# Matmuls that read their moving operand alternately from the two halves of its tile

## The chip, the core and the metric

The kernel runs on one core of a Trainium2 chip. The metric is the device time of one execution in microseconds (us); the kernel before was run three times. A core has five engines that work side by side and wait for each other through semaphores: TensorE (PE; its weight loads, PEld, overlap its matmuls), VectorE (DVE), ScalarE (ACT), GpSimd (POOL) and SyncE (SP), which here issues all transfers. Matmul results go to PSUM, eight banks of 512 float32 values in each of 128 partitions; all other tiles lie in SBUF.

## What is computed

A two-layer network on 1024 tokens with 1024 channels, in float32. Layer 0 mixes with sliding-window attention, layer 1 with a gated linear recurrence (HGRN2); a squared-ReLU feed-forward part follows each.

```python
def sqrelu_mlp(h, w_up, w_down):
    return jnp.square(jax.nn.relu(h @ w_up)) @ w_down

def reference(x, positions, ...):
    ...
    for layer in range(DEPTH):
        h = rmsnorm(x, mix_norm[layer])
        if layer % N_MIXERS == 0:
            y = sliding_window_attention(h, positions, ...)   # h @ w_qkv + b, rotary, band of 128, @ w_o
        else:
            y = hgrn2_recurrence(h, lbs[layer], ...)          # h @ w_in, scan over chunks, @ w_o
        x = x + y
        h = rmsnorm(x, mlp_norm[layer])
        x = x + sqrelu_mlp(h, mlp_w_up[layer], mlp_w_down[layer])
    return rmsnorm(x, final_norm)
```

The feed-forward weights are 1024 x 4096 and 4096 x 1024, the recurrence's input weights 1024 x 4096.

## The kernel before

**Layout.** Activations are held transposed: a tile has 128 channels on the partitions and 512 tokens (half of the 1024, index `hf`) in the free dimension. Weights come in blocks of 128 x 512 (`wr`).

**Products in three parts.** A large product is done in float32r, a form of float32 that TensorE takes with fewer bits. `weight_split` and `split` cut each operand into a high part (a cast) and a low part (the difference), and `mm3` adds three matmuls in one PSUM bank: high x high, high x low and low x high. In most products the weights are the stationary operand (128 x 128, names `wh` and `wl`) and the activations the moving one (128 x 512, names `a` or `t`); in the qkv projection it is the other way round, and there the bank has tokens on its partitions and the 512 output channels as its columns.

**Fewer products.** Up projection, down projection and the recurrence's input projections are 2 x 2 block products in the form with seven products (`strassen_weights`, `finish`, `operands`); `product` runs one with 4 x 3 matmuls. Partial sums stay in a bank and are read in between: by ScalarE (`copy`) into a tile, or by VectorE, which adds a bank to a tile (`tt`). Such reads stand in `pair` (up), `down`, `two` and `two_first` (gates of the recurrence), `o_proj`, `hgrn_out`, `projected` and `keys_values` (qkv). PSUM banks have two tags, `q` and `p`, four banks each.

**The last part.** `down` of the last layer ends with products of 256 tokens at a time, and `final` normalises and stores each quarter as it comes; for such a quarter two tiles of 256 columns go out with one transfer.

**What sets the order.** No engine's order is written by hand. `Schedule.add` records each operation with a cost, and `Schedule.order` plays them through as a list scheduler: of what is ready, the operation of the lowest rank on the engine that is free first. Casts that split operands may go to ScalarE or VectorE, whichever the planner takes to end first. The cost of a matmul is set in `mm` (for 512 columns of float32r: 512 / 2.25 + 4 = 231.6). All operations are issued from one place, so every row of the profile has the same line, and the tiles' names tell them apart: `wr` raw weights, `m` sums of weights, `wh` and `wl` split weights, `a` and `t` activations, `d` a store in DRAM, `q` and `p` PSUM banks, `c` constants.

Of the kernel before, what the change touches and what calls it, by code (L numbers as in the profile page):

```python
# [275 lines left out]


class Net:
    def __init__(self, ctx, tc, io):
# [152 lines left out]
    def sum_squares(self, tiles, n=TH):  # L432
        acc = None
        for x in tiles:
            sq = self.t()[:, :n]
            self.act(sq, x, AF.Square, n)
# [49 lines left out]
    def square_relu(self, m, hf, c, psum):  # L486

        r = self.t()
        if psum:
            self.act(r, c, AF.Relu)  # L490
            self.stt(r, c, 0.0, r, ALU.max, ALU.mult)
        else:
            self.stt(r, c, 0.0, c, ALU.max, ALU.mult)
        self.hid[m, hf] = self.keep(r)
# [86 lines left out]
    def pair(self, m, x):  # L581

        w = self.strassen_weights(*(self.io["up"][self.layer, i] for i in (m, m + MT // 2)))

        def read(ps):
            z = self.t()
            self.copy(z, ps)
            return z

        main, side, own = self.psum("q"), self.psum("q"), self.psum()  # L590
        self.product(main, w[1], x[1], True)
        u1 = read(main)
# [11 lines left out]
        self.tt("DVE", u2, side, u2, ALU.add)  # L604
# [56 lines left out]
    def down(self, cut):  # L661
# [8 lines left out]

        def products(names, ps, ws, start, stop, tokens=slice(0, TH), ms=range(HK)):
            for p in ps:
                for name in names:
                    (wh, wl), (xh, xl) = ws[name, p]
                    for m in ms:
                        out = (main if name in (1, 6, 7, 4) else side)[m][:, tokens]
# [3 lines left out]
                        self.mm3(out, (wh[:, c], wl[:, c]), (xh[:, tokens], xl[:, tokens]), first, p == stop,  # L680
                                 tokens.stop - tokens.start, **more)

# [10 lines left out]

        def scaled_sum(hf, out, z, tokens=slice(0, TH)):

            k = tokens.stop - tokens.start
            u = self.t(tag="m")[:, :k]
            self.tt("DVE", u, z, self.r[hf][:, tokens], ALU.mult, k)
            part = out[:, tokens].only(tokens.start)
            self.tt("any", part, u, part, ALU.add, k)  # L700
# [7 lines left out]
        for m in range(HK):  # L708
            y[0, 0, m], y[1, 1, m] = self.a(), self.a()
            self.copy(y[0, 0, m], main[m])  # L710
        for m in range(HK):
            self.copy(y[1, 1, m], side[m])
        run_pass((6,))
        for m in range(HK):
            u = y[0, 1, m] = self.a()
            self.copy(u, main[m])
        for m in range(HK):
# [3 lines left out]
        for m in range(HK):  # L721
            self.copy(parts[m], main[m])
        for m in range(HK):
# [13 lines left out]
        for m in range(HK):  # L737
            self.copy(parts[m], side[m])
        for m in range(HK):
# [16 lines left out]
        for c in (0, TH // 2):  # L756
            tokens = slice(c, c + TH // 2)
            for m in range(HK):
                products((3,), range(n - held, n), ws, False, n - 1, tokens, [m])
                scaled_sum(1, self.x[m][1], side[m][:, tokens], tokens)  # L760
            yield 1, tokens

# [90 lines left out]
    def projected(self, cg, n, ps, r):  # L853
        if cg == 0:
            self.keys_values(n, ps, r)
        else:
            q = self.a()
            self.stt(q, ps, r, self.bias[cg], ALU.mult, ALU.add)
            self.rope(q, 8, n)
            self.q[n][cg - 1] = q  # L860

    def keys_values(self, n, ps, r):
        W = NG * HD
        k = self.t(F32, (P, W))
        self.stt(k, ps[:, :W], r, self.bias[0][:, :W], ALU.mult, ALU.add, W)
        if n % 2 == 0:
            self.v.append(self.a(F32, (P, 2, W)))
        v = self.v[n // 2][:, n % 2].only(n)
        self.stt(v, ps[:, W:], r, self.bias[0][:, W:], ALU.mult, ALU.add, W)
        if n % 2 == 0:  # L870
# [101 lines left out]
    def o_proj(self, hf, out):  # L972

        a = [self.split(out[g, j]) for g in range(NG) for j in range(2)]
        for m in range(KT):
# [6 lines left out]
            self.x[m][hf] = self.a()  # L982
            self.tt("DVE", self.x[m][hf], ps, x, ALU.add)
            yield
# [61 lines left out]
    def two_first(self, which, e, x):  # L1046

        self.s.lead = LEAD
        w = [self.weight_split(self.raw(self.io["win"][which[0], e][:, c : c + TH])) for c in (0, TH)]
        self.s.lead = 0  # L1050
        main, own, y0 = self.psum(), self.psum(), self.t()
        self.product(main, w[0], x[1], True)
        self.copy(y0, main)
        self.product(own, w[1], x[2], True)
        self.tt("DVE", y0, own, y0, ALU.add)
        return main, y0

    def two(self, which, e, x, out, begun=None):
# [6 lines left out]
        if not begun:  # L1065
            self.product(main, w[1], x[1], True)
            self.copy(y0, main)
        yield
        self.product(side, w[5], x[5], True)
        self.copy(z1, side)  # L1070
        yield
        self.product(main, w[6], x[6], False)
        self.copy(y1, main)
        yield
        if not begun:
            self.product(own, w[2], x[2], True)
            self.tt("DVE", y0, own, y0, ALU.add)
        yield
        self.product(main, w[7], x[7], False)
        self.tt("DVE", z1, main, z1, ALU.add)  # L1080
        yield
        self.product(side, w[3], x[3], False)
        self.tt("DVE", y1, side, y1, ALU.add)
        yield
        self.product(main, w[4], x[4], False)
        self.copy(z0, main)
        yield
# [132 lines left out]
    def hgrn_out(self, hf, y, total):  # L1220
        r = self.t()
        self.copy(r, self.rstd(total, 0.25, 0.25))
        for m in range(KT):
# [6 lines left out]
            z = self.t()  # L1230
            self.tt("DVE", z, ps, r, ALU.mult)
            self.x[m][hf] = self.a()
# [31 lines left out]

    def final(self, hf, tokens=slice(0, TH)):
        n = tokens.stop - tokens.start
        xs = [self.x[kt][hf][:, tokens].only(tokens.start) for kt in range(KT)]
        r, rs = self.rstd(self.sum_squares(xs, n), n=n), self.t()[:, :n]
# [3 lines left out]
        for k in range(0, KT, per):  # L1272
            pair = self.a().rearrange("p (k t) -> p k t", k=per)
            for kt in range(k, k + per):
                y = pair[:, kt - k].only(kt)
                if kt < 2:
                    self.act(y, xs[kt], AF.Copy, n, scale=self.gain(4, kt))
                    self.tt("Pool", y, y, rs, ALU.mult, n)
                else:
                    self.stt(y, xs[kt], self.gain(4, kt), r, ALU.mult, ALU.mult, n)  # L1280
            self.dma(self.io["out"][hf, k : k + per, :, tokens].rearrange("k p t -> p k t"), pair, 4 * P * TH)
        self.s.lead = 0
# [92 lines left out]
```

## Time and profile before

| what | value |
|---|---|
| three runs | 2179.08, 2181.03, 2183.65 us; median 2181.03 |
| profiled execution, first to last instruction (span) | 2174.9 us, 32278 instructions |
| all that the three runs' median has beyond that span | 6.1 us |
| mean granted TensorE clock | 0.994 |
| DMA | 316.49 MB, mean 146 GB/s |

The page lists no time of the profiled execution but its span; the median of the runs is 6.1 us longer. In the profile "busy" is the time in which an engine has an instruction at work. Matmuls overlap: a matmul of 512 columns is shown with about 394 ns, and the next one starts before its end, so TensorE's rate is read from the distance between starts. VectorE's instructions overlap a little too. The stages, by the trace's time: qkv of the first half to 80 us, attention and output projection to 310, up projection of layer 0 from about 340 to 640, down projection to about 1000, recurrence to about 1400, its output projection to 1540, up projection of layer 1 to 1800, down projection and output to the end.

### The profile page before, as it was taken

To read this page: it belongs to the slowest core of one execution; us is meant where nothing else is said; L and a number is where in the kernel's file an instruction comes from. 1 tells how busy PE (TensorE), PEld (TensorE's weight loads), DVE (VectorE), ACT (ScalarE), POOL (GpSimd) and SP (SyncE) were. 2 spreads that over 40 slices of the span, in tenths; PEclk is the share of its full clock that TensorE was granted. 3 is DMA by queue.
4 is the path that set the end of the run, shared out by engine and by line. 5 is a ranking of instruction groups with operands and counts; after the bars stand their busy time and mean duration, and the time that the engine had idled before them with its cause. 6 is when DMAs were issued, how large, how long until landed. Compare 5 with 4: busy or idle time off the path is not lost.

```text
span 2174.9 us, 32278 instructions
## 1 busy us (share of the span) xinstructions
PE 2129.5 (98%) x11374; PEld 1713.3 (79%) x11374; DVE 1823.6 (84%) x3608; ACT 837.7 (39%) x1757; POOL 62.4 (3%) x124
## 2 busy tenths in 40 slices
PE   8999999999999999999999999999999999999997
PEld 6777778888877887877788888878788887888786
DVE  8899889667789888899888888878976678988887
ACT  5567755122234233365333333343521223322442
POOL 4030000000000000000100000000000000000000
PEclk9999999999999999999999999999999999999999
DMA  6212363333369867741111111547333336976652
GB/s 204 75 48 83 112 194 116 105 109 111 108 204 305 274 202 234 247 136 49 56 57 59 58 53 52 188 148 227 113 114 103 107 116 224 305 241 226 209 171 78
DMA packets 174274, 316.49 MB, mean 146 GB/s; under 512 B 19616, under 2 KB 21664, under 8 KB 174112
## 3 DMA queue, kind: packets, MB, share of 16 engines
q1 hardware_dynamic: 174112, 314.43, 44.7%
q8 instruction: 89, 1.46, 0.3%
q14 instruction: 73, 0.60, 0.1%
HBM read 250.39 MB, written 63.96 MB: 145 GB/s over the span
## 4 chain that ended last, share of the span: by engine, by line
PE 85%; DVE 7%; ACT 4%; DMA 2%; issue 1%; SPq 0%; DVEq 0%; ACTq 0%
PE q L326 45%; PE p L326 40%; DVE a L326 3%; DVE t L326 2%; ACT t L326 1%; ACT a L326 1%; DVE wl L326 1%; DVE m L326 1%; DMA wr<-in_down 1%; ACT m L326 1%; ACT wh L326 0%; DMA t<-d 0%; DVE wh L326 0%; DMA d<-t 0%; DMA a<-d 0%
## 5 line engine op out<-in xcount | busy, mean ns | idle before, releaser
L326 PE MATMUL q<-a,wh 128*128 128x512 f32 x2560 | 798.6, 395 | 5.0 <-DVE t L326 2.3
L326 PE MATMUL p<-a,wh 128*128 128x512 f32 x2336 | 754.4, 402 | 9.1 <-ACT t L326 3.7
L326 PEld LDWEIGHTS q<-a,wh 128*128 128x128 f32 x2560 | 480.1, 188 | 120.5 <-ACT t L326 4.1
L326 PEld LDWEIGHTS p<-a,wh 128*128 128x128 f32 x2336 | 432.0, 189 | 107.7 <-ACT t L326 4.6
L326 PE MATMUL q<-a,wl 128*128 128x512 f32 x1280 | 499.5, 394 | 0.0
L326 PE MATMUL p<-a,wl 128*128 128x512 f32 x1168 | 462.8, 397 | 0.0
L326 PEld LDWEIGHTS q<-a,wl 128*128 128x128 f32 x1280 | 240.4, 188 | 56.6
L326 PEld LDWEIGHTS p<-a,wl 128*128 128x128 f32 x1168 | 220.4, 189 | 50.5 <-issue 0.5
L326 DVE TENSOR_TENSOR wl<-wr,wh 128x512 fp32r<-128x512 f32 x352 | 241.0, 686 | 15.5 <-ACT wh L326 5.4
L326 ACT COPY t<-q 128x512 f32<-128x512 f32 (+2 forms) x201 | 111.8, 562 | 349.0 <-PE q L326 344.1
L326 DVE TENSOR_TENSOR a<-t,a 128x512 fp32r<-128x512 f32 (+1 forms) x294 | 195.0, 685 | 0.8 <-DMA t<-d 0.5
L326 DVE CAST wh<-wr 128x512 fp32r<-128x512 f32 x204 | 87.8, 430 | 127.6 <-PE p L326 78.4
L326 DVE TENSOR_TENSOR wl<-m,wh 128x512 fp32r<-128x512 f32 x256 | 176.3, 689 | 16.1 <-ACT wh L326 6.1
L326 ACT CAST wh<-m 128x512 fp32r<-128x512 f32 x153 | 95.2, 623 | 210.4 <-PE q L326 148.4
L326 DVE TENSOR_TENSOR t<-t,t 128x512 f32<-128x512 f32 (+3 forms) x268 | 159.7, 611 | 17.7 <-DMA t<-d 10.7
L326 ACT CAST a<-t 128x512 fp32r<-128x512 f32 x189 | 114.7, 619 | 128.8 <-PE q L326 82.6
L326 ACT CAST wh<-wr 128x512 fp32r<-128x512 f32 x148 | 91.1, 619 | 172.7 <-PE p L326 109.3
L326 PE MATMUL p<-wh,a 128*128 128x512 f32 x384 | 130.6, 407 | 8.2 <-ACT a L326 7.0
L326 DVE TENSOR_TENSOR m<-wr,wr 128x512 f32<-128x512 f32 x160 | 109.7, 687 | 22.2 <-DMA wr<-in_down 11.9
L326 PEld LDWEIGHTS q<-t,t 128*64 128x64 f32 (+1 forms) x2160 | 98.0, 144 | 25.0 <-issue 11.2
L326 PE MATMUL q<-t,t 128*64 128x32 f32 (+2 forms) x2160 | 111.5, 230 | 0.0
L326 DVE CAST wh<-m 128x512 fp32r<-128x512 f32 x103 | 44.3, 430 | 73.4 <-PE q L326 59.7
(117 smaller groups left out, 2113.9 us busy)
## 6 DMA issues: line engine op xcount, KB each, us to landing
t<-d SPq DMA_DIRECT2D x296, 256.0 KB, 4.7
wr<-in_down SPq DMA_DIRECT2D x256, 256.0 KB, 3.9
d<-t SPq DMA_DIRECT2D x180, 256.0 KB, 2.4
wr<-in_up SPq DMA_DIRECT2D x128, 256.0 KB, 2.9
wr<-in_win SPq DMA_DIRECT2D x68, 256.0 KB, 2.9
a<-d SPq DMA_DIRECT2D x60, 256.0 KB, 4.4
wr<-in_wqkv SPq DMA_DIRECT2D x48, 256.0 KB, 2.8
d<-a SPq DMA_DIRECT2D x48, 256.0 KB, 2.4
```

What stands on the lines that cost most here:

```text
L326: fn(*[place(a) for a in args], **{k: place(v) for k, v in kw.items()})
```

## The change

Three functions give views of a tile of 2n columns. `turned` lists the columns as 0, n, 1, n + 1 and so on; `straight` undoes that for a bank that was filled in this order; `halves` shows a tile as two halves.

- **The moving operand.** `mm3` reads both parts of the moving operand through `turned`: of 512 columns one of the first half (1 KB) and one of the second half in turn. The number of matmuls, their columns and their stationary operands stay. For the products of 256 columns `cols` picks 256 of the turned columns: 128 neighbouring tokens of each half.
- **The banks.** A bank of `mm3` then holds its columns in the turned order. Whoever reads one reads it with a step of two elements (`straight`) and writes the tile in the plain order (`halves`): `take` for copies, `add_bank` for sums, and the same in `square_relu`, `scaled_sum`, `projected`, `keys_values` and `hgrn_out`. In `keys_values` the even columns of the bank are keys and the odd ones values.
- **The end.** The last quarters are then 128 tokens from each half, so `final` works on views of two pieces and stores each pair of tiles with two transfers instead of one.
- **The planner's cost.** A matmul's cost is n x rate / 2.4 + 3 for every kind: 216.3 for 512 columns.

```diff
+def turned(z):
+    return z.rearrange("p (a b) -> p b a", a=2)
+def straight(z):
+    return z.rearrange("p (b a) -> p a b", a=2)
+def halves(z):
+    return z.rearrange("p (a b) -> p a b", a=2)
...
-        cost = n * rate / (2.25 if rate == 1.0 else 2.4) + 4
+        cost = n * rate / 2.4 + 3
...
-    def mm3(self, out, w, x, start, stop, n=TH, **kw):
+    def mm3(self, out, w, x, start, stop, n=TH, cols=slice(0, TH), **kw):
         (wh, wl), (xh, xl) = w, x
+        xh, xl = (turned(z)[:, cols.start // 2 : cols.stop // 2] for z in (xh, xl))
         self.mm(out, wh, xh, start, False, n, **kw)
...
+            c, h = straight(c), halves(r)
+            self.act(h, c, AF.Relu)
+            self.stt(h, c, 0.0, h, ALU.max, ALU.mult)
...
+    def take(self, out, bank):
+        self.copy(halves(out), straight(bank))
+    def add_bank(self, z, bank, to=None):
+        self.tt("DVE", halves(z if to is None else to), straight(bank), halves(z), ALU.add)
...
-            self.copy(z, ps)
+            self.take(z, ps)
...
-        self.tt("DVE", u1, own, u1, ALU.add)
+        self.add_bank(u1, own)
...
+            k, piece = cols.stop - cols.start, slice(cols.start // 2, cols.stop // 2)
+            u = halves(self.t(tag="m")[:, :k])
+            z = straight(z[:, cols]) if z.buf.tag in "pq" else halves(z)
+            self.tt("DVE", u, z, halves(self.r[hf])[:, :, piece], ALU.mult, k)
+            part = halves(out)[:, :, piece].only(cols.start)
             self.tt("any", part, u, part, ALU.add, k)
...
-            self.stt(q, ps, r, self.bias[cg], ALU.mult, ALU.add)
+            self.stt(halves(q), straight(ps), r, halves(self.bias[cg]), ALU.mult, ALU.add)
...
-            self.dma(self.io["out"][hf, k : k + per, :, tokens].rearrange("k p t -> p k t"), pair, 4 * P * TH)
+            to = self.io["out"][hf, k : k + per].rearrange("k p t -> p k t")
+            if n == TH:
+                self.dma(to, pair, 4 * P * TH)
+                continue
+            for a in range(2):
+                c, h = a * TH // 2, slice(a * n // 2, (a + 1) * n // 2)
+                self.dma(to[:, :, c + piece.start : c + piece.stop], pair[:, :, h], 2 * P * TH)
```

With the new cost the planner moves some rows. On TensorE 83% of the matmuls keep their place in the row and none moves by more than 51 places. In the up projection of layer 0 (function `pair`, one pair of row blocks, its split weights and the reads of its banks), VectorE's rows before are these, with `m1241` the weight sum of the third product:

```order
L326 TENSOR_TENSOR m1275_5062<-wr1273_4990,wr1274_5033 128x512
L326 TENSOR_TENSOR m1276_5069<-m1275_5062,wr1271_4913 128x512
L326 TENSOR_TENSOR m1278_5076<-wr1272_4970,m1276_5069 128x512
L326 TENSOR_TENSOR wl1251_5085<-m1241_4917,wh1250_5078 128x512
L326 SCALAR_TENSOR_TENSOR t1232_5083<-q1219_4884,t1232_5083 128x512
L326 TENSOR_TENSOR wl1253_5102<-m1240_4851,wh1252_5092 128x512
```

In the changed kernel the same place on VectorE reads:

```order
L341 TENSOR_TENSOR m1275_5063<-wr1273_4990,wr1274_5033 128x512
L341 TENSOR_TENSOR m1276_5070<-m1275_5063,wr1271_4914 128x512
L341 CAST wh1250_5077<-m1241_4923 128x512
L341 TENSOR_TENSOR m1278_5082<-wr1272_4970,m1276_5070 128x512
L341 TENSOR_TENSOR wl1251_5087<-m1241_4923,wh1250_5077 128x512
L341 SCALAR_TENSOR_TENSOR t1232_5079<-q1219_4884,t1232_5079 128x512
L341 TENSOR_TENSOR wl1253_5101<-m1240_4853,wh1252_5094 128x512
```

The cast that makes `wh1250`, on ScalarE before, now stands on VectorE, once in each pair. The second place is SyncE's queue at the very end, the last stores of the output (`a` tiles of two channels' blocks), before:

```order
L326 DMA out<-a_21674 128x512
L326 DMA out<-a_21827 128x2x256
L326 DMA out<-a_21612 128x2x256
L326 DMA out<-a_21840 128x2x256
L326 DMA out<-a_21861 128x2x256
```

and in the changed kernel:

```order
L341 DMA out<-a_21725 128x512
L341 DMA out<-a_21846 128x2x128 x2
L341 DMA out<-a_21608 128x2x128 x2
L341 DMA out<-a_21865 128x2x128 x2
L341 DMA out<-a_21876 128x2x128 x2
```

Each store of a quarter became two of half its size.

More of the change, by code (lines that the diff above doesn't have):

```diff
@@ L669, in down, with products @@
         side = [self.psum() for m in range(HK)]
-        def products(names, ps, ws, start, stop, tokens=slice(0, TH), ms=range(HK)):
+        def products(names, ps, ws, start, stop, cols=slice(0, TH), ms=range(HK)):
             for p in ps:
@@ L679, in products @@
                         first = p == 0 and not more
-                        self.mm3(out, (wh[:, c], wl[:, c]), (xh[:, tokens], xl[:, tokens]), first, p == stop,
-                                 tokens.stop - tokens.start, **more)
+                        self.mm3(out, (wh[:, c], wl[:, c]), (xh, xl), first, p == stop, cols.stop - cols.start, cols, **more)
         def run_pass(names, held=0):
@@ L715, in down @@
             u = y[0, 1, m] = self.a()
-            self.copy(u, main[m])
+            self.take(u, main[m])
         for m in range(HK):
@@ L721, in down @@
         for m in range(HK):
-            self.copy(parts[m], main[m])
+            self.take(parts[m], main[m])
         for m in range(HK):
@@ L737, in down @@
         for m in range(HK):
-            self.copy(parts[m], side[m])
+            self.take(parts[m], side[m])
         for m in range(HK):
@@ L982, in o_proj @@
             self.x[m][hf] = self.a()
-            self.tt("DVE", self.x[m][hf], ps, x, ALU.add)
+            self.add_bank(x, ps, self.x[m][hf])
             yield
@@ L1052, in two_first @@
         self.product(main, w[0], x[1], True)
-        self.copy(y0, main)
+        self.take(y0, main)
         self.product(own, w[1], x[2], True)
-        self.tt("DVE", y0, own, y0, ALU.add)
+        self.add_bank(y0, own)
         return main, y0
@@ L1230, in hgrn_out @@
             z = self.t()
-            self.tt("DVE", z, ps, r, ALU.mult)
+            self.tt("DVE", halves(z), straight(ps), halves(r), ALU.mult)
             self.x[m][hf] = self.a()
```

61 lines of the change are left out of this document (29 added, 32 removed).

## The prediction

> **What bounds the kernel now.** I read the page's totals first, then the chain that ended last, then the groups of matmuls, and last the busy times by stretch.
>
> ```profile
> span 2174.9 us, 32278 instructions
> PE 2129.5 (98%) x11374; PEld 1713.3 (79%) x11374; DVE 1823.6 (84%) x3608; ACT 837.7 (39%) x1757; POOL 62.4 (3%) x124
> ...
> PEclk9999999999999999999999999999999999999999
> ...
> PE 85%; DVE 7%; ACT 4%; DMA 2%; issue 1%; SPq 0%; DVEq 0%; ACTq 0%
> ```
>
> TensorE is busy through the whole span, at the full granted clock (nine tenths or more in each slice), and holds 85% of the chain. VectorE comes next with 84% busy. What counts is then the distance between the starts of two matmuls. In the up projections the chain goes from pair to pair in equal steps; the third row is from a pass of the down projection (start, us, work).
>
> ```profile
> 403.10 16.70 PE q L326 x72
> ...
> 422.58 16.70 PE q L326 x72
> ...
> 742.39 35.89 PE q L326 x155
> ```
>
> A pair of row blocks has 7 products of 12 matmuls, 84, and takes 422.58 - 403.10 = 19.48 us: 231.9 ns each. The pass gives 35.89 / 155 = 231.5 ns. I take 231.7 ns for a float32r matmul of 512 columns. These are the groups (count | busy us, mean ns):
>
> ```profile
> L326 PE MATMUL q<-a,wh 128*128 128x512 f32 x2560 | 798.6, 395 | 5.0 <-DVE t L326 2.3 <-ACT t L326 1.8 <-ACT wh L326 0.9
> L326 PE MATMUL p<-a,wh 128*128 128x512 f32 x2336 | 754.4, 402 | 9.1 <-ACT t L326 3.7 <-ACT wh L326 3.2 <-DVE t L326 1.4
> L326 PE MATMUL q<-a,wl 128*128 128x512 f32 x1280 | 499.5, 394 | 0.0
> L326 PE MATMUL p<-a,wl 128*128 128x512 f32 x1168 | 462.8, 397 | 0.0
> L326 PE MATMUL p<-wh,a 128*128 128x512 f32 x384 | 130.6, 407 | 8.2 <-ACT a L326 7.0 <-ACT wh L326 1.2
> L326 PE MATMUL p<-wl,a 128*128 128x512 f32 x192 | 77.3, 403 | 0.0
> L326 PE MATMUL p<-a,a 128*128 128x512 f32 x48 | 11.4, 395 | 0.0
> ```
>
> Together 2560 + 2336 + 1280 + 1168 + 384 + 192 + 48 = 7968 matmuls, all of which `mm3` makes: 7968 x 231.7 ns = 1846 of the 2175 us.
>
> **What the turned read could change.** Is 231.7 ns what the array needs, or what its feed allows? Three other kinds of matmul answer (start, us, work; merged rows end with the drain of the last one):
>
> ```profile
> 194.33 1.03 PE L326 MATMUL q<-c,a 128*128 128x128 f32 x8
> ...
> 608.77 1.88 PE L326 MATMUL q<-t,c 128*128 128x512 f32 x4
> ...
> 2137.80 1.35 PE L326 MATMUL p<-a,a 128*128 128x256 f32 x10
> ```
> ```profile
> L326 PE MATMUL p<-a,a 128*128 128x256 f32 x192 | 24.3, 285 | 0.0
> ...
> L326 PE MATMUL q<-c,a 128*128 128x128 f32 x64 | 9.3, 275 | 0.3
> L326 PE MATMUL q<-t,c 128*128 128x512 f32 x18 | 9.0, 597 | 0.3 <-DVE t L326 0.3
> ```
>
> The float32r matmuls of 256 columns start (1.35 - 0.285) / 9 = 118 ns apart, half of 231.7: the time goes with the columns, so it is neither an issue cost nor the weight load, which has 128 columns in both. The plain float32 matmuls of 512 columns (the spread of a norm) start (1.88 - 0.597) / 3 = 428 ns apart, which is 1.85 times 231.7. The transposes of 128 columns start (1.03 - 0.275) / 7 = 108 ns apart, 1.86 times 231.7 / 4 = 57.9. If plain float32 is streamed twice, one pass of 512 columns takes 214 ns by the first and 4 x 108 / 2 = 216 ns by the second. So the array can take 512 columns in about 216 ns, and the once-streamed float32r operand loses 15.7 ns. A feed that can't bring one new 4-byte column in each array step fits that: the twice-streamed kinds need half as much new data per step.
>
> [...]
>
> Whether reading from the two halves in turn, 1 KB apart, lifts the feed, no row shows, for every operand of 512 columns is read straight now. From above it is bounded by 214 ns, from below by the price of a read that suits the store worse: in the recurrence some VectorE operations work on short runs of 4-byte elements, and their rows give a price.
>
> ```profile
> 1085.96 0.74 DVE L326 COPY_PREDICATED t<-c,q 128x256 f32<-128x256 int32 x1
> 1086.50 1.46 DVE L326 TENSOR_TENSOR t<-t,t 128x256 f32<-128x256 f32 x4
> ...
> 1090.01 0.73 DVE L326 COPY_PREDICATED t<-c,q 128x256 f32<-128x256 int32 x1
> ...
> 1097.07 0.43 DVE L326 COPY_PREDICATED t<-c,q 128x256 f32<-128x256 int32 x1
> 1097.40 1.43 DVE L326 TENSOR_TENSOR t<-t,m 128x256 f32<-128x256 f32 x4
> ```
>
> The predicated copies are of levels 0, 1 and 2: runs of one, two and four elements. One and two cost 0.74 and 0.73 us, four 0.43. The four products behind them (level 0: every second element; level 2: runs of four) take 1.46 and 1.43 us, so there the step costs nothing. One kind pays 1.72 times, one nothing. I take 216 ns: the matmul rows are nearest, and an operand with a constant step is closer to the products than to a copy under a mask.
>
> **The sum.** On TensorE's stream alone the saving is 7968 x 15.7 ns = 125.1 us, and 192 matmuls of 256 columns x (118 - 108) ns = 2 us. Only what lies on the chain shortens the span, if the order stays. 85% of 2174.9 is 1849 us. Off it go the matmuls in q banks that aren't turned (attention, recurrence); these rows are the chain's shares for 80 to 310, 1000 to 1400 and 1400 to 1540 us:
>
> ```profile
> by line: PE p L326 38.3%; PE q L326 25.6%; ACT a L326 6.6%; ACT m L326 5.7%; DVE t L326 5.1%; ACT t L326 4.6%; DVE a L326 4.4%; issue 2.6%; DVE m L326 2.2%; DVE wl L326 2.2%; ACT wh L326 1.0%; DVE wh L326 0.7%; ACT L326 0.6%; DVE sm L326 0.
> ```
> ```profile
> by line: PE p L326 70.2%; PE q L326 24.7%; DVE t L326 1.9%; DVE m L326 1.0%; issue 0.7%; ACT t L326 0.6%; ACT L326 0.3%; DVE wl L326 0.3%; DVE wh L326 0.2%; ACT wh L326 0.1%
> ```
> ```profile
> by line: PE p L326 50.5%; PE q L326 15.5%; DVE t L326 7.8%; DVE a L326 5.8%; ACT t L326 5.3%; DVE wl L326 3.5%; issue 3.3%; DVE m L326 2.8%; ACT a L326 2.1%; DMA wr<-in_wg 1.8%; ACT wh L326 0.8%; DVE wh L326 0.6%; ACT m L326 0.2%; DVE sm L3
> ```
>
> That is 0.256 x 230 + 0.247 x 400 + 0.155 x 140 = 179 us. Left are 1670 us, or 7207 matmuls, x 15.7 ns = 113.1 us, and the 2 us at the end.
>
> VectorE is next. Its back-to-back rate and three stretches (busy PE, PEld, DVE, ACT, POOL):
>
> ```profile
> 335.49 2.49 DVE L326 TENSOR_TENSOR a<-t,a 128x512 fp32r<-128x512 f32 x4
> ```
> ```profile
> 310.00:360.00 50.00, 49.96 (x220) 40.38 (x219) 47.16 (x84) 26.68 (x49) 0.00 (x0) 1.00 0.37 121
> 360.00:600.00 240.00, 240.00 (x1037) 194.47 (x1037) 173.72 (x299) 51.22 (x90) 0.00 (x0) 1.00 0.35 112
> ...
> 920.00:1000.00 80.00, 73.50 (x300) 58.20 (x300) 74.35 (x158) 50.32 (x93) 0.36 (x2) 0.94 0.34 110
> 1000.00:1400.00 400.00, 398.59 (x3277) 321.20 (x3276) 353.41 (x800) 146.60 (x303) 9.14 (x16) 1.00 0.21 67
> ```
>
> From 310 to 360 VectorE starts an operation about every 0.60 us ((2.49 - 0.68) / 3) and is busy 47.16 of 50 us; 220 matmuls would save 3.5 us and leave it 46.5. From 920 to 1000 it has 74.35 of 80 us, and some 4.6 us would go. I count both savings, 8 us, as lost to VectorE. In the up projections (173.72 of 240) it has room: the cast that the planner moves there from ScalarE to VectorE in each pair, 0.43 us in the row below, lies beside 84 x 216 ns = 18.1 us of matmuls. Were VectorE full there, 32 pairs would pay 14 us.
>
> ```profile
> L326 DVE CAST wh<-m 128x512 fp32r<-128x512 f32 x103 | 44.3, 430 | 73.4 <-PE q L326 59.7 <-PE p L326 13.7
> L326 ACT COPY t<-q 128x512 f32<-128x512 f32 x175 | 102.2, 586 | 338.9 <-PE q L326 338.3 <-DVE a L326 0.5
> ```
>
> Banks read with a step of 2: 264 ScalarE reads (per pair 4 copies and a relu, 40 copies in the two down projections, 64 in the gates) and, in whole banks, 216 VectorE reads (96 in the pairs, 12 in the down projections, 48 in the gates, 48 in the qkv, output and gated projections, 12 for the 24 half reads) are between nothing (the products) and 0.62 us more for a bank (twice 0.74 - 0.43). I take nothing, since reading is what the products do; the other end is a rival. ScalarE's 264, at most doubled (0.586 us each, the second row), add 155 us to an engine with 61% idle.
>
> At the end the last eight stores become sixteen, of which four more come after the last norm.
>
> ```profile
> 2.11 3.96 SPq L326 DMA_DIRECT2D a<-in_x x8
> ```
>
> An issue takes 3.96 / 8 = 0.5 us; four cost up to 2 us and partly hide behind the arithmetic that feeds them: 1 us.
>
> The profiled execution: 2174.9 - 113.1 - 2 + 8 + 1 = 2068.8 us of span. The median of the runs, 2181.03, lies 6.1 us above the span before, so I add that: **2075 us**.
>
> **The rivals.**
> - *The reads of the banks pay.* At 0.62 us each VectorE gets 134 us more. In the gates 48 x 0.62 = 30 us come to 353.41 of 400 us, while the 816 + 409 matmuls of the rows below would save 19: VectorE needs 383, and the stage gains nothing. With the output and gated projections (16 x 0.62 = 10 us each) and the ends of the down projections some 45 us are given back: 2120 us. For it: the predicated copies. Against it: the products.
> - *The feed doesn't depend on the addresses.* Then 231.7 ns stay, and a reordering of few rows and 1 us at the end are left: 2181 us. For it: the distance is the same in an up projection and a down pass, and no row has another address order. Against it: the 256-column rows, which rule out weight loads and issue, leave little but the operand's read.
> - *The turned read is slower.* Successive columns come from places 1 KB apart, so no two neighbours share a run. If the moving operand pays like the predicated copies, 1.72 times, a matmul takes 399 ns and 7968 x 167 ns = 1331 us come on top: about 3510 us. It decides from 232 ns up: each ns costs 8 us. For it: those copies. Against it: the products, and that the read alternates between two straight streams.
>
> ```profile
> L326 PE MATMUL p<-a,wh 128*128 128x512 f32 x816 | 267.2, 407 | 0.5 <-ACT t L326 0.4
> L326 PE MATMUL p<-a,wl 128*128 128x512 f32 x409 | 161.5, 396 | 0.0
> ```
>
> [...]
>
> **How the numbers follow.** Forecast 0.76, bank reads 0.08, no effect 0.06, slower read 0.10. A measurement of this kernel can tell about 0.2% (4.4 us) from no change. So faster 0.84, within 0.2% 0.06, slower 0.10. The low end is the whole stream's saving, 127 us, with 214 to 215 ns a matmul (8 us more): 2046. The high end takes in most of the bank reads: 2125.
>
> **What would show it.** A pair of the up projection at 18.1 us instead of 19.48; the plain float32 rows unchanged; copies out of q banks still at 586 ns and VectorE's reads of p banks at 683, as in the row below; VectorE's share near 88%, with TensorE waiting for it at 310 to 360 and 920 to 1000 us. A pair at 19.5 or above, or bank reads longer by some 0.3 us or more, would make the prediction wrong; so would chain parts of VectorE, ScalarE and DMA that grow by more than the 8 us.
>
> ```profile
> L326 DVE TENSOR_TENSOR t<-p,t 128x512 f32<-128x512 f32 x96 | 65.4, 683 | 1.2 <-PE p L326 1.1
> ```

## The result, and the profile after

| | before | after |
|---|---|---|
| median of the runs, us | 2180.06 (4 runs) | 2074.94 (4 runs; 2071.18 to 2081.45) |
| ratio of the times | | 0.9519, 95% interval 0.9501 to 0.9538 |
| span of the profiled execution, us | 2174.9 | 2073.1 |

The profiled execution of the changed kernel took 2074.85 us in all, 1.75 us more than its span. The spans differ by 101.8 us, the medians by 105.1: the profiled execution of the kernel before was a short one (other executions of it with a span of 2174.9 us took 2176.7). The totals, the clock and the chain of waits on the page of the changed kernel:

```profile
span 2073.1 us, 32285 instructions
...
PE 2008.0 (97%) x11374; PEld 1721.5 (83%) x11374; DVE 1809.6 (87%) x3598; ACT 841.5 (41%) x1767; POOL 63.6 (3%) x124
...
PEclk9999999999999999999999999999999999999998
...
PE 81%; DVE 13%; ACT 3%; DMA 2%; issue 2%; SPq 0%; DVEq 0%; ACTq 0%
```

The same matmuls run, and TensorE still bounds the kernel. Its step is shorter. The chain in the up projection of layer 0 (start, us, work):

```profile
402.38 15.54 PE q L341 x72
417.92 2.59 PE p L341 x12
420.50 15.54 PE q L341 x72
```

A pair takes 420.50 - 402.38 = 18.12 us, 215.7 ns for each of 84 matmuls, where it took 19.48. The busy times of three stretches (PE, PEld, DVE, ACT, POOL); the first and the last hold the matmuls of 512 columns that stood from 310 to 360 and from 920 to 1000 us before:

```profile
297.33:344.07 46.74, 46.48 (x220) 40.30 (x218) 44.34 (x75) 28.22 (x50) 0.00 (x0) 1.00 0.40 127
360.00:600.00 240.00, 240.00 (x1110) 209.42 (x1109) 185.47 (x329) 47.08 (x82) 0.00 (x0) 1.00 0.39 124
870.20:950.20 80.00, 68.18 (x309) 57.69 (x308) 78.44 (x168) 52.50 (x97) 0.36 (x2) 0.94 0.39 130
```

From 360 to 600 us stand 1110 matmuls instead of 1037. In the first row TensorE is busy nearly throughout. In the last it is busy 68.18 of 80 us and VectorE 78.44: here TensorE now waits. Most of that is one gap in the timeline of TensorE, ahead of a pass of the down projection, where the kernel before waited 3.30 us (at 990 us, for ScalarE):

```profile
936.09 1.22 PE L341 MATMUL p<-a,wh 128*128 128x512 f32 x2 [10.14 <-ACT wh L341]
```

To see where the gain arises I numbered the 7968 matmuls of 512 columns in both traces and compared the starts of every 250th. Where TensorE runs without a break, 250 of them took 57.9 us before and 54.0 after. In four pieces nothing was gained: numbers 750 to 1000 (70.9 us before, 72.1 after), 3000 to 3250 (58.6, 58.4), 3500 to 3750 (70.9, 71.2) and 5000 to 5250 (79.6, 80.2). Before, they began at 276, 815, 931 and 1417 us, at changes of stage or from one pass of the down projection to the next.

Two counts from the starts of the matmuls recur below. **Waits** are the time by which the gap between two starts exceeds the usual 232 or 216 ns, where it is over 0.47 us (behind a smaller matmul the whole gap, where it is over 0.9 us). **Half-speed loss** is the excess of gaps of 0.38 to 0.47 us, which come in rows behind long waits (in the second run 0.43 us apart behind a wait of 3.46 us). Before, they are 38.4 and 6.9 us; after, 56.7 and 11.7.

### The profile page after: what moved, and what is told of

The parts are those of the page before. It is cut to its first block, busy times and chain, and to the rows that moved or that the text cites. A ratio compares the mean times of both kernels' runs of the same rounds, so it can differ in the third digit from the quotient of the medians.

```text
span 2073.1 us, 32285 instructions
## 1 busy us (share of the span) xinstructions
PE 2008.0 (97%) x11374; PEld 1721.5 (83%) x11374; DVE 1809.6 (87%) x3598; ACT 841.5 (41%) x1767; POOL 63.6 (3%) x124
## 3 DMA queue, kind: packets, MB, share of 16 engines
q8 instruction: 89, 1.46, 0.3%
## 4 chain that ended last, share of the span: by engine, by line
PE 81%; DVE 13%; ACT 3%; DMA 2%; issue 2%; SPq 0%; DVEq 0%; ACTq 0%
PE q L341 46%; PE p L341 35%; DVE a L341 5%; DVE t L341 4%; DVE m L341 2%; DVE wl L341 1%; ACT t L341 1%; ACT a L341 1%; DMA wr<-in_down 1%; DMA a<-in_x 0%; DVE sm L341 0%; ACT wh L341 0%; DMA a<-d 0%; DMA wr<-in_up 0%; ACT m L341 0%
## 5 line engine op out<-in xcount | busy, mean ns | idle before, releaser
L341 PE MATMUL q<-a,wh 128*128 128x512 f32 x2560 | 761.0, 381 | 11.1 <-ACT t L341 7.1
L341 PE MATMUL p<-a,wh 128*128 128x512 f32 x2336 | 720.8, 387 | 14.5 <-ACT wh L341 11.8
L341 PE MATMUL q<-a,wl 128*128 128x512 f32 x1280 | 482.0, 380 | 0.3 <-DVE wl L341 0.3
L341 PE MATMUL p<-a,wl 128*128 128x512 f32 x1168 | 447.2, 384 | 0.0
L341 ACT CAST a<-t 128x512 fp32r<-128x512 f32 x198 | 119.6, 618 | 121.7 <-PE q L341 54.6
L341 ACT CAST wh<-m 128x512 fp32r<-128x512 f32 x145 | 89.7, 620 | 140.9 <-PE q L341 82.6
L341 PE MATMUL p<-wh,a 128*128 128x512 f32 x384 | 122.0, 389 | 9.5 <-DVE c L341 8.0
L341 ACT CAST a<-a 128x512 fp32r<-128x512 f32 x111 | 67.9, 621 | 85.1 <-DVE a L341 44.8
```

Source lines behind the costliest of these rows:

```text
L341: fn(*[place(a) for a in args], **{k: place(v) for k, v in kw.items()})
```

## The experiments

Three questions: does the turned read alone make the step shorter, and why? Are the bank reads free? And what is the planner's new cost worth, which the prediction counted at nothing?

**1. The new cost alone, on the kernel before.**

```diff
-        cost = n * rate / (2.25 if rate == 1.0 else 2.4) + 4
+        cost = n * rate / 2.4 + 3
```

> The kernel before with nothing changed but the planner's cost of a matmul (n x rate / 2.4 + 3); operands and banks are read straight. Theory A (the gain is the turned read; the new order is worth nothing): 2176 to 2186 us, a pair of the up projection still 19.5 us. Rival B (part of the 105 us comes from a better order): some 10 us or more below 2180, pairs still 19.5 us.

Measured 2177.76 us, ratio 0.9985 (0.9976 to 0.9994). Its chain in the up projection:

```profile
417.58 16.69 PE q L326 x72
...
437.07 16.70 PE q L326 x72
```

The pair stays at 437.07 - 417.58 = 19.49 us. With straight reads the new order is worth some 3 us.

**2. The changed kernel with the old cost.** The same line, the other way round.

> The changed kernel with the old planner's cost (n / 2.25 + 4), so nearly the old order. Theory A: within 5 us of 2075, a pair of the up projection 18.1 us. Rival B (the order that fits the faster matmul matters): 2085 us or more, with longer waits of TensorE in the stretches where VectorE is full.

Measured 2111.18 us, ratio 0.9686 (0.9669 to 0.9704). The chain in the up projection, then the totals and the chain's shares on its page:

```profile
411.44 15.54 PE q L341 x72
...
429.57 15.54 PE q L341 x72
```
```profile
PE 2029.7 (96%) x11374; PEld 1729.4 (82%) x11374; DVE 1820.4 (86%) x3608; ACT 834.1 (40%) x1757; POOL 63.7 (3%) x124
...
PE 67%; DVE 17%; DMA 8%; ACT 4%; issue 4%; SPq 0%; DVEq 0%; ACTq 0%
```

The pair is as short as in the changed kernel, 18.13 us, yet the kernel takes 36 us more. So the read does what it does whatever the order, and the cost's 36 us lie elsewhere: in the chain TensorE has 67% instead of 81%. By the numbers of the matmuls, this kernel and the changed one run equally fast from 1250 to 2250 (54.0 us per 250 up to 2000); this one is 8 us behind at number 1000, 19 at 3250, 29 at 7250, 35 at 7500. It loses at the changes of stage and between passes of the down projections. Its waits are 75.9 us (56.7 in the changed kernel) and its half-speed loss is 21.6 (11.7), together 29 of the 36 us; the rest is not placed. One place in its timeline, at the end of the up projection of layer 0:

```profile
632.32 1.22 PE L341 MATMUL q<-a,wh 128*128 128x512 f32 x2 [3.46 <-DVE t L341]
633.34 0.63 PE L341 MATMUL q<-a,wl 128*128 128x512 f32 x1
633.77 1.06 PE L341 MATMUL p<-a,wh 128*128 128x512 f32 x2
...
638.55 0.59 PE L341 MATMUL q<-a,wh 128*128 128x512 f32 x2
```

and the same place in the changed kernel:

```profile
621.09 0.70 PE L341 MATMUL q<-a,wh 128*128 128x512 f32 x2 [1.05 <-DVE t L341]
621.63 0.38 PE L341 MATMUL q<-a,wl 128*128 128x512 f32 x1
```

With the old cost TensorE waits 3.46 us for VectorE instead of 1.05, and then the matmuls start 0.43 us apart (633.77 - 633.34) for some 5 us, half the usual speed. Later rows have one every 0.216 us again. The granted clock, the third number from the end in the rows below, was 0.50 meanwhile (first row; 1.00 from 639 us). The second row is from the changed kernel:

```profile
634.00:637.00 3.00, 3.00 (x8) 2.37 (x8) 2.13 (x5) 1.59 (x4) 0.00 (x0) 0.50 1.00 320
787.00:790.00 3.00, 3.00 (x9) 2.37 (x8) 3.00 (x6) 2.14 (x5) 0.00 (x0) 0.50 0.95 322
```

So this wait was paid twice. How long a wait must be for that is not shown, and its length alone does not decide: in the changed kernel waits of 2.51 us (at 786 us, the second row above) and 2.06 us (at 1759 us) were followed by a clock of 0.50 too, while after one of 2.14 us (at 1468 us) it stayed at 1.00.

**3. The bank reads alone.** Old cost and straight moving operand; the bank reads with a step of two and the split stores of the end stay.

```diff
-        xh, xl = (turned(z)[:, cols.start // 2 : cols.stop // 2] for z in (xh, xl))
+        xh, xl = (z[:, cols] for z in (xh, xl))
```

> Old cost, moving operand read straight, but every bank read with a step of 2 and the last stores in two pieces, as in the changed kernel. The columns of each product thus land in another order than they are used in, so the function computed is another one with the same work. Theory A (bank reads are free, the end costs about 1 us): 2178 to 2185 us, ScalarE's copies out of q banks 585 ns, VectorE's sums 683 ns. Rival C (the step costs, and the changed kernel hides it): 2190 us or more, or copies and sums longer by 50 ns or more.

Measured 2180.15 us, ratio 1.0002 (0.9993 to 1.0011). The two groups of bank reads (count | busy us, mean ns | idle time before):

```profile
L341 ACT COPY t<-q 128x512 f32<-128x512 f32 x175 | 102.2, 586 | 340.7 <-PE q L341 340.1 <-DVE a L341 0.5
...
L341 DVE TENSOR_TENSOR t<-p,t 128x512 f32<-128x512 f32 x96 | 65.3, 683 | 1.6 <-PE p L341 1.2 <-issue 0.2
```

586 and 683 ns are what straight reads took before. The step costs nothing on either engine in these rows, and all of it together, stores included, makes no difference that can be measured. The gain needs the turned moving operand.

**4. Address patterns by themselves.** Sixteen groups of 48 float32r matmuls of 512 columns (the first of 96), each with another view of one moving tile.

```diff
+    views = [
+        lambda z: z,
+        lambda z: z.rearrange("p (a b) -> p b a", a=2),
+        lambda z: z.rearrange("p (k a b) -> p k b a", a=2, k=2),
...
+        lambda z: z.rearrange("p (b a) -> p a b", a=2),
...
+        lambda z: z.rearrange("p (a b) -> p b a", a=4),
+        lambda z: z.rearrange("p (a b c) -> p b a c", a=2, c=2),
...
+        for k in range(96 if i == 0 else 48):
+            w = weights[:, k % 4 * P : k % 4 * P + P]
+            net.mm(ps, w, view(moving), k == 0, k == (95 if i == 0 else 47))
```

> None of the network is computed: sixteen groups of 48 float32r matmuls of 512 columns on the same operands (the first has 96), each group with another order of the moving operand's columns, and each group's bank copied out. Theory D (contiguous reading has neighbours that collide, and any second stream far enough away avoids it): straight 231.7 ns at both ends; two columns in turn 1 KB, 512 B, 256 B and 128 B apart 216 ns; from some smaller distance (64 B or 16 B) on back to 231.7 ns. [...] Rival F (what helps is only that neighbours in time are not neighbours in place): every order but the straight one, a plain step of 2, 4 and 16 among them, takes 216 ns.

The timeline of TensorE, in the order of the groups: two streams 1 KB apart (first row below), 16 bytes apart, 8 bytes apart, one stream with a step of two, four streams, runs of two columns from each half, runs of four, and straight:

```profile
35.34 10.52 PE L326 MATMUL q<-a,wh 128*128 128x512 f32 x48
...
97.50 10.52 PE L326 MATMUL q<-a,wh 128*128 128x512 f32 x48
107.86 11.08 PE L326 MATMUL p<-a,wh 128*128 128x512 f32 x48
118.78 21.91 PE L326 MATMUL q<-a,wh 128*128 128x512 f32 x48
...
183.46 13.77 PE L326 MATMUL p<-a,wh 128*128 128x512 f32 x48
197.07 16.18 PE L326 MATMUL q<-a,wh 128*128 128x512 f32 x48
213.07 12.17 PE L326 MATMUL p<-a,wh 128*128 128x512 f32 x48
225.08 11.09 PE L326 MATMUL q<-a,wh 128*128 128x512 f32 x48
```

From start to start, per matmul of a group's steady part: 215.8 ns for all seven distances from 1 KB down to 16 bytes; 226.7 at 8 bytes and straight; 453 for a step of two (461 and 433 for steps of 4 and 16); 283, 333 and 250 for four streams and for runs of two and of four. So it isn't the distance that helps, nor that the tile is read in two halves. Nor does every order other than the straight one help: single steps take about twice as long. A reading that fits the streams and the steps, inferred from these figures alone: the even and the odd columns of the operand's order are fetched by two readers, each of which gets 16 bytes at a time. In the straight order each reader would use two 4-byte columns of every 16 bytes (226.7 ns); with two streams at least 16 bytes apart all four (215.8 ns); with a step of two only one (453 ns). The four streams and the runs of two (one column at a time per reader) and of four (two) don't follow from this count: they took 283, 333 and 250 ns, not 453, 453 and 227.

**5. That reading, tested.** Groups that change the use of each 16 bytes and little else.

```diff
+    groups = [
+        [one],
...
+        [half(one)],
+        [wide[:, : 2 * TH].rearrange("p (a b s) -> p b a s", a=2, s=2)[:, :, :, 0]],
+        [wide.rearrange("p (a b s) -> p b a s", a=2, s=4)[:, :, :, 0]],
+        [wide[:, : TH // 2].unsqueeze(2).to_broadcast([P, TH // 2, 2])],
...
+        [runs(8)],
...
+        [hi, lo, hi],
+        [half(hi), half(lo), half(hi)],
```

> None of the network is computed: groups of 48 float32r matmuls of 512 columns, as in the first such run. Theory J (even and odd columns come through two readers, and each is at full speed when it finds all four values of a 16-byte line in a row, a little slower with two, at half speed with one): halves 216 ns; two streams 1 KB apart each with a step of 2, 228 ns; each with a step of 4, 430 ns or more; every column read twice 216 ns; one stream with a step of 2, 430 ns or more; halves 4 KB apart 216 ns; runs of 8, 16 and 64 of each half in turn between 250 and 228 ns, falling to 228 as the runs grow. Rival D (any second stream far enough away avoids a collision of neighbours): two streams 216 ns with a step of 2 and of 4 as well, and runs of 64 near 216. The groups that change operand and weights from matmul to matmul, as the network does, tell whether the straight read's 231.7 ns there, against 228 in the first such run, comes from that: 231 to 232 if so, 228 if not; turned 216 either way.

Straight, halves, two streams each with a step of two, the same with a step of four, every column twice, and halves 4 KB apart:

```profile
35.01 11.04 PE L326 MATMUL q<-wide,wh 128*128 128x512 f32 x48
45.89 10.52 PE L326 MATMUL p<-wide,wh 128*128 128x512 f32 x48
56.25 11.08 PE L326 MATMUL q<-wide,wh 128*128 128x512 f32 x48
67.17 21.91 PE L326 MATMUL p<-wide,wh 128*128 128x512 f32 x48
88.90 10.54 PE L326 MATMUL q<-wide,wh 128*128 128x512 f32 x48
...
120.92 10.54 PE L326 MATMUL q<-wide,wh 128*128 128x512 f32 x48
```

That is 226.7, 215.8, 226.7, 453.4, 215.8 and 215.8 ns. Two streams with a step of two (two columns of each 16 bytes per reader) cost what the straight read costs, with a step of four (one column) twice that, and 4 KB is as good as 1 KB. These are the figures of the two-reader reading, and a second stream that merely lies far away is not enough. Runs of 8, 16 and 64 columns took 243.4, 240.0 and 226.7 ns: they fall towards the straight read as expected, but a count of columns per 16 bytes alone would give 227 for all. That the engine is built so is an inference; what is shown are the figures. In the plain order of the columns the turned read never takes two of the same 16 bytes in a row, and it is the fastest; the reading has to count the even and the odd columns apart, and then one column of each 16 bytes goes with 453 ns, two with 226.7 and four with 215.8.

**6. Too low and too high a cost.** The planner of the changed kernel is told 193 ns for a matmul that takes 216, and that of the kernel before 248 ns for one that takes 232.

```diff
-        cost = n * rate / 2.4 + 3
+        cost = n * rate / 2.7 + 3
...
-        cost = n * rate / (2.25 if rate == 1.0 else 2.4) + 4
+        cost = n * rate / (2.1 if rate == 1.0 else 2.4) + 4
```

> The changed kernel with the planner's cost of a matmul too low: n x rate / 2.7 + 3, 193 ns for 512 columns that take 216. With the cost 7% too high the same kernel took 2111 us. Theory G (the plan has to have the right cost, on either side): 2085 us or more. Theory H (only a cost that is too high hurts: the planner then lets VectorE and ScalarE work be late, and TensorE waits): 2068 to 2082 us.

> The kernel before, straight reads, with the planner's cost too high by the same 7%: n / 2.1 + 4, 248 ns for 512 columns that take 231.7. Theories G and H: 2200 us or more, with TensorE waits of over 3.5 us and matmuls at 460 ns behind them. Rival I (the 36 us that the old cost lost belong to the faster matmul, which leaves VectorE less slack, not to the wrong cost): 2175 to 2188 us.

Too low: 2076.4 us, ratio 0.952 (0.9507 to 0.9534), the same as the changed kernel. Too high: 2219.38 us, ratio 1.0175 (1.016 to 1.019), 38.6 us more than before. TensorE's longest waits in the latter (us in all, times, longest):

```profile
PE q L326 <- DVE t L326: 18.0, 9, 4.2
PE q L326 <- ACT wh L326: 7.1, 2, 6.2
```

Its waits come to 68.6 us (38.4 before) and its half-speed loss to 15.8 (6.9), 39.1 us more in all. So a cost 7% above the truth costs some 36 to 39 us whichever way the operand is read, and one 11% below costs nothing that can be measured, though TensorE's waits rise from 56.7 to 65.0 us with it. The direction is shown; why is argued from the planner's code: told that TensorE is slow, it ranks side work on VectorE and ScalarE later than TensorE needs it.

**7. The planner's lead.** `LEAD` ranks the preparation of weights (their loads, sums and splits) so many places earlier.

```diff
-LEAD = 100
+LEAD = 140
```

> The changed kernel with weights planned a little earlier (LEAD 140 instead of 100), tried as a better version: what is left of TensorE's waits (57 us, against 38 before) would shrink if weight splits come too late in the stretches where VectorE and ScalarE are full. If so: 2060 to 2070 us. If those stretches are bound by VectorE's work itself: within 5 us of 2075.

> The changed kernel with a lead of 180 places in place of 100 (140 gave 2067.84 us, 7 us less than the changed kernel). Theory H (what is left of the transition losses comes from side work that is planned too late): 2058 to 2068 us, TensorE's waits below 50 us. Rival (the lead runs out of what it can move, or takes buffers too early): 2068 to 2080 us.

> The kernel before with the planner's lead for the marked operations at 140 places in place of 100, straight reads and the old cost. Theory L (a longer lead is worth some us whichever way the operand is read, as the too-high cost hurt both): 3 to 8 us less than before, ratio 0.996 to 0.9985. Rival M (the lead pays only because the turned read shortened TensorE's work, so that the others' must start earlier by rank): within 2 us of before or slower.

The changed kernel took 2067.84 us with 140 (ratio 0.9494, 0.9473 to 0.9515) and 2079.39 with 180 (0.9525, 0.9505 to 0.9546); the kernel before took 2187.12 with 140 (1.0028, 1.0014 to 1.0042). There is no trend: 140 is the fastest kernel of the study, but its interval overlaps the changed kernel's, with 180 the gain is gone, and before it costs 6 us. Where 140 gains is mostly one stretch, numbers 3500 to 3750, with 63.4 us instead of 71.2: the wait of 10.14 us shown above is gone there. A new order seems to move these kernels by some 6 us either way. Of the theories behind these runs, that a longer lead helps both kernels fell; that what is left of the waits shrinks with it held at 140 (50.7 us) and not at 180 (55.8).

**8. Why 231.7 ns in the network and 226.7 alone?** In the fifth run a straight group that changes operands and weights from matmul to matmul, as the network does, took 226.7 ns too. Next a run with company (VectorE, ScalarE, DMA stores) and with other starts (`at(4)` begins at column 4):

```diff
+    groups = [
+        (at(0), ""), (at(0), ""), (at(1), ""), (at(2), ""), (at(3), ""), (at(4), ""), (at(8), ""),
+        (half(at(1)), ""), (half(at(2)), ""),
+        (at(0), "V"), (at(0), "A"), (at(0), "D"), (at(0), "VAD"), (half(at(0)), "VAD"),
+        (far, ""), (at(0), ""),
+    ]
```

> A microbenchmark that computes nothing of the network: after a warm-up of 96, groups of 48 float32r matmuls of 512 columns, with the same high/low/high operands as the network. Groups: straight; straight from a start 1, 2, 3, 4 and 8 elements further on; turned halves from a start 1 and 2 elements further on; straight beside 15 VectorE operations, beside 15 ScalarE copies, beside 12 DMA stores, beside all three; turned beside all three; straight at the far end of the tile; straight. The question is why the straight read costs 231.7 ns in the network and 226.7 ns alone. Theory B (the other engines' or the DMAs' traffic takes it): one of the groups with company stands at 230 to 233 ns, all others straight at 226.7. Theory S (the start address decides): a straight group with an offset stands at 230 or more, the company changes nothing. Theory N (neither): 226.7 ns in every straight group; the 5 ns then stay open. [...]

Straight, from columns 1, 4 and 8, then beside all three and turned beside all three:

```profile
33.92 11.04 PE L326 MATMUL q<-wide,wh 128*128 128x512 f32 x48
44.80 11.52 PE L326 MATMUL p<-wide,wh 128*128 128x512 f32 x48
...
78.34 11.28 PE L326 MATMUL q<-wide,wh 128*128 128x512 f32 x48
89.46 11.36 PE L326 MATMUL p<-wide,wh 128*128 128x512 f32 x48
...
154.09 11.04 PE L326 MATMUL p<-wide,wh 128*128 128x512 f32 x48
164.97 10.52 PE L326 MATMUL q<-wide,wh 128*128 128x512 f32 x48
```

Company changes nothing (226.7 straight, 215.8 turned), the start does: 236.7, 233.3, 228.9, 231.7 and 233.3 ns from columns 1, 2, 3, 4 and 8, but 216.6 and 216.0 turned (from columns 1 and 2). Loads were not among the company, but in the trace before the matmuls start 231.3 ns apart from 760 to 780 us, where the DMA moves 31 GB/s, and 231.7 from 700 to 720 us, where it moves 309. By the program's addresses, which no view here shows, most tiles of the network start 32 bytes off a multiple of 64. So the last run padded them, told the planner 226.7 ns and read straight:

```diff
+        if pool is None and n * 4 % 64 and (len(shape) == 2 or n == 130):
+            wide = [P, -(-n // 16) * 16] if len(shape) == 2 else [P, shape[1], n + 2]
+            v = self.s.tile(self.pool, bufs, wide, dt, tag, f"{tag}{self.n}")
+            return v[:, :n] if len(shape) == 2 else v[:, :, :n]
...
-        cost = n * rate / (2.25 if rate == 1.0 else 2.4) + 4
+        cost = n * rate / 2.4 + (13.4 if rate == 1.0 else 4)
```

> The kernel before with straight reads, but every tile padded so that it starts at a multiple of 64 bytes (before, three quarters of the moving operands start 32 bytes off such a multiple, as do nearly all weights), and the planner told 226.7 ns for a matmul. In the run with offsets a straight matmul took 226.7 ns from an aligned start and 228.9 to 236.7 ns from the others, and company changed nothing. Theory S (the start addresses of operand and weights make the network's 231.7 ns): 226.7 to 228 ns apart, a pair at 19.05 to 19.15 us, and 5 ns x 7207 = 36 us less: 2140 to 2150 us. Rival N (it is something else that only the network has, for instance that each tile is used only a few times; the network's own matmuls, sorted by the start of their operand, differ by 1 ns only): a pair at 19.45 to 19.5 us, 2174 to 2184 us. Theory H, on the cost, adds nothing here, since the cost fits whichever holds within 2%.

Measured 2176.84 us, ratio 0.9985 (0.9972 to 0.9998). The chain in the up projection:

```profile
420.57 16.61 PE q L331 x72
437.19 2.79 PE p L331 x12
439.97 16.67 PE q L331 x72
```

The pair takes 19.40 us, 231.0 ns a matmul. If the padding aligned every tile, as the edit means to, aligned starts don't give the 226.7 ns, and the rival holds. What in the network costs the other 5 ns stays open; turned reads don't pay it, there or alone.

## Why the prediction was right, and where its steps were not

**The read, right.** It rested on one pass of 512 columns in transposes and plain float32 matmuls: 216 and 214 ns, against 231.7. That these kinds are streamed twice was the author's estimate from the ratios 1.86 and 1.85; no run tests it by itself. Measured 215.7. The mechanism it offered, a feed that can't bring one new 4-byte column in each step, fits the column read twice (215.8 ns in the fifth run) but not the turned read itself, which brings as many new columns as the straight one and takes 215.8 ns against 226.7: there the order of the addresses decides, not the amount of new data. Before the runs no row showed that, and the prediction gave it 0.76. Plain float32 matmuls were to stay as they were, and did (1.88 us for four). Of the matmuls of 256 columns it expected 108 ns; the trace shows about 112 (in the row below (3.40 - 0.28) / 28 = 111), so a little less than the 2 us was had there.

```profile
2030.30 3.40 PE L341 MATMUL p<-a,a 128*128 128x256 f32 x29
```

**The bank reads, right.** They were taken as free, because VectorE's products with a step of two cost nothing (1.46 us for four, 1.43 with runs of four), against the predicated copies (0.74 us against 0.43). The third run shows it by itself for copies and sums, and the changed kernel's copies and sums have the old durations (585 and 683 ns):

```profile
L341 ACT COPY t<-q 128x512 f32<-128x512 f32 x175 | 101.9, 585 | 306.4 <-PE q L341 305.1 <-DVE a L341 1.0
...
L341 DVE TENSOR_TENSOR t<-p,t 128x512 f32<-128x512 f32 x96 | 65.3, 683 | 2.4 <-PE p L341 1.3 <-ACT t L341 1.0
```

So the rivals of paid bank reads, of a feed that doesn't depend on addresses and of a slower turned read are out. The last was not far off in kind: a read with a step of two does cost 453 ns. Two streams are spared that price (215.8 ns), as the prediction said against this rival.

**The sum, right as a total, wrong in one step.** The span was to fall by 106.1 us and fell by 101.8. The failed step is "Only what lies on the chain shortens the span, if the order stays", with the cost's reordering given no worth. The second run is nearly that case: turned reads, old cost. It saves 70 us of the medians, not 105. With an unchanged cost the planner believes in slower matmuls than there are, and 36 us are lost, 29 of them in longer waits and the slow matmuls behind them. The new cost gave these 36 us back. The cost alone is worth 3 us, the read alone 70, both together 105: some 32 us need both.

**The lost part, right in one of two places, too small in size.** 8 us were to go where VectorE is full, from 310 to 360 and from 920 to 1000 us. The same matmuls can be found by number in both traces. Those of 310 to 360 us took 49.9 us before and 46.7 after: 3.1 us came there, nearly all that the shorter step gives 210 matmuls. Those of 920 to 1000 us took 80.0 both times, so all 4.6 us were lost. The rest was lost where the prediction had counted none: of what the step gives, 6 us are missing from 1400 to 1540, 4 from 640 to 920 and 7 from 1800 to the end (times before). From the other side: the stream's 126.7 us (7968 x (231.7 - 215.8) ns) less 18.3 us of added waits and 4.8 of added half-speed loss leaves 103.6, against 101.8 between the spans.

**The number, near by luck.** The prediction came near the span because it also left out 12 us of matmuls that it saw off the chain (125.1 - 113.1). They did count: from 80 to 310 us, where the chain gives TensorE only 64%, the 553 matmuls saved 10.0 us, more than the step alone gives (8.8). A missing loss and a missing gain cancelled. The last cancelling is plain luck: the span came out 4.3 us above the forecast (2073.1 against 2068.8), and the 6.1 us added to it for the median came out at 1.8, since most of the 6.1 was a short profiled execution before. So 2075 met 2074.94.

**Its own test, badly chosen.** It said that chain parts of VectorE, ScalarE and DMA growing by more than 8 us would make it wrong. VectorE's share rose from 7 to 13%, some 117 us more, and the time came out as forecast. Where TensorE and VectorE are both nearly full, the chain may run through either, and a share of it is no added time. The waits of TensorE are the better test (us in all, times, longest; after). Before, the first two kinds came to 9.8 and 4.4 us; the last row is the wait at the start, 7.0 us before:

```profile
PE q L341 <- DVE t L341: 13.6, 9, 4.9
PE p L341 <- ACT wh L341: 13.3, 3, 10.1
PE q L341 <- ACT t L341: 9.8, 12, 2.5
PE p L341 <- DVE c L341: 8.0, 1, 8.0
```

## What to carry to other kernels

Before believing that an engine is at its limit, compare kinds of the same instruction that feed it differently: here the transposes in the same trace (108 ns for 128 columns), counted as streamed twice, pointed to the 16 ns that the turned read then took off each matmul. When an instruction gets faster, tell the planner in the same change; a cost that is too high loses at the changes of stage, and one that is too low lost nothing here. Check a forecast by the time that the same instructions take before and after and by the waits of the bounding engine, not by shares of the chain.

## What the runs showed of the hardware that was not expected

- The rate of a float32r matmul of 512 columns depends on the order of its columns' addresses: 215.8 ns for two alternating straight streams 16 bytes to 4 KB apart, 226.7 straight (231.7 in the network), 250 for runs of four, 283 for four streams, 333 for runs of two, 433 to 461 for single streams with steps of 2, 4 and 16.
- A straight read from another start took up to 236.7 ns; a turned one, from columns 1 and 2, at most 216.6.
- Reads of a float32 PSUM bank with a step of two cost ScalarE (586 ns for 128 x 512) and VectorE (683 ns) nothing: straight ones took 586 and 683 before.
- VectorE, ScalarE and 12 stores at work beside the matmuls did not slow either kind of read (226.7 and 215.8 ns).
- After a wait of 3.46 us in the second run the matmuls ran at half speed for some 5 us, 0.43 us apart, at a granted clock of 0.50. In the changed kernel the clock was 0.50 after one wait of 2.06 us and stayed at 1.00 after one of 2.14 us.
